# A Conformer/RWKV-7 block: the depthwise convolution's taps given a place of their own in the order of work

## The chip, the cores and the metric

The kernel runs on one core of a Trainium2 chip. The metric is the device time of one execution in microseconds. Matmuls run on TensorE (PE; PEld is its weight load), the element-wise work on VectorE (DVE), ScalarE (ACT) and GpSimd (POOL), and SyncE (SP) issues the transfers. PE has two clocks, 1.2 and 2.4 GHz; the trace's granted clock is 1.00 at the higher one.

## What is computed

One hybrid layer in float32 for a sequence of 512 and a width of 1024: a convolution branch, a recurrent branch (RWKV-7, 16 heads of 64), gates that merge them, and a feed-forward part.

```python
h = modulate(rms_norm(x, g_norm1), shift1, scale1)
u = h @ w_in
u_conv, u_rwkv, u_gate = jnp.split(u, [2 * CONV_DIM, 2 * CONV_DIM + RWKV_COLS], axis=-1)
y_conv = conformer_conv(u_conv, ...)
y_rwkv = rwkv7_mix(u_rwkv, ...)
g_conv, g_rwkv = jnp.split(jax.nn.sigmoid(u_gate), N_BRANCH, axis=-1)
merged = g_conv * y_conv + g_rwkv * y_rwkv
x = x + gate1[:, None, :] * (merged @ w_out)
h2 = modulate(rms_norm(x, g_norm2), shift2, scale2)
ff = jnp.square(jax.nn.relu(h2 @ w_ff1)) @ w_ff2
return x + gate2[:, None, :] * ff

def conformer_conv(u, conv_w, conv_b, ln_g, ln_b, w_pw, b_pw):
    za, zb = jnp.split(u, 2, axis=-1)
    z = za * jax.nn.sigmoid(zb)
    z = depthwise_causal_conv(z, conv_w, width=31) + conv_b
    z = jax.nn.silu(layer_norm(z, ln_g, ln_b))
    return z @ w_pw + b_pw

def step(S, inp):
    r_t, w_t, k_t, v_t, a_t, b_t = inp
    Sa = jnp.einsum('bhij,bhj->bhi', S, a_t)
    S = S * w_t[:, :, None, :] + Sa[..., None] * b_t[:, :, None, :] + v_t[..., None] * k_t[:, :, None, :]
    return S, jnp.einsum('bhij,bhj->bhi', S, r_t)
```

(The convolution call is shortened to its meaning.)

## The kernel before, in words

Activations lie with channels on the partitions, in blocks of 128 channels by 512 positions. Every weight product goes through `wload` and `wmul` (lines 211 to 226): SP loads 128 columns of a weight matrix (`raw`, line 213), ACT rounds them to a high part (`wH`, line 215), POOL takes the rest (`wL`, line 216), and PE makes 24 matmuls (lines 223, 224, 225), three for each of eight slices of 128, into one of three PSUM accumulators `mm`. These are called dense matmuls here, and 24 of them a block.

The recurrence is cut into 8 chunks of 64 positions and handled for 4 groups of 4 heads. For a group come, in this order: `group_k` and `group_prep` (its r, k, v and decays, and the products of a chunk's rows among themselves, lines 546 to 698, with `group_bonus`, line 701); `group_solve` (lines 704 to 736), which inverts triangles in 31 steps of two small dependent DVE operations each (lines 721, 723), ending in DVE's transpose `G.solved`; `group_solve2` (line 738), with the matmuls `sW` and `sX` (lines 747, 753); `group_chain` (line 758), the eight steps that hand the state on: matmuls `pf` (lines 767, 769), ACT's copy F (772), matmuls `pu` (776), two copies to UV, on ACT (778) and DVE (779), matmuls `pn` (784), DVE's `sp` and S (791, 792); and `group_post`. The outputs Y (lines 799, 801) stand beside the steps.

The convolution goes by 8 blocks of 128 channels. `conv_in(j)` (line 513) makes two dense blocks and the gated input `z` (three buffers; line 520 on DVE takes it from PSUM). `conv_taps(j, z)` (line 523) makes the 31 taps through `weighted_sum` (line 133): ACT writes the first tap with the bias into one PSUM accumulator `acc` (line 143), 30 DVE operations add the others (line 145), the result is stored to DRAM (line 527), and `csum` adds up the blocks for the layer norm that follows in the stage "norm" (lines 889 to 908; its root and reciprocal are lines 198 and 199).

What orders the work is a scheduler with priorities: an instruction gets its priority from its place in the program's text, `forward(section, g)` (lines 72 to 83) shifts a section by the number in the table `FORWARD`, and of the instructions that are ready each engine gets the one with the best priority; each engine then runs its list strictly in that order. `tc.issue_after(x)` holds work back until `x` stands in the order. `window` (line 857) hands out what fills the groups, by the table `WINDOWS` (line 23): "c" is a conv block, "g" a gate block, and the bar separates what stands before a group's chain from what stands behind its start. Blocks 0 and 1 of the convolution have their inputs before the first group.

## Time and profile before

| | |
|---|---|
| median of 3 runs | 1150.29 us (1146.22 to 1151.23) |
| profiled execution | 1150.57 us, span 1148.8 us |
| granted clock of PE, mean | 0.969 |
| PE busy | 1066.7 us (93% of the span) |
| DVE busy | 765.2 us (67%) |
| ACT busy | 494.8 us (43%) |
| POOL busy | 429.5 us (37%) |

The span is the time from the first to the last instruction in the trace of one execution. In the view of busy time by stage a row has the stretch, its length, then for PE, PEld, DVE, ACT and POOL the busy us with the number of instructions in brackets, then the granted clock, the share of the transfer engines and the GB/s. A row of the timeline has the start in us, the duration in us, the engine, the line, the operation, out<-in with the tiles' names, and their shapes; "x8" at its end means that eight like it are put together, and a bracket tells how long the engine had been idle and what ended that. The copies of a tile have numbers in the order of instructions, which the trace leaves out.

### The profile page before, as it was taken

Reading aid. Unit: us, or ns where it says so; the run is one execution under the profiler, and the core shown is the slowest. Engines: PE = TensorE matmul, PEld = TensorE weight load, DVE = VectorE, ACT = ScalarE, POOL = GpSimd, SP = SyncE. Lnnn points to the kernel's source line nnn. Section 1 sums busy time; section 2 is a strip of 40 time slices with the busy share of each in tenths; the row PEclk is TensorE's granted clock in tenths of the full one; section 3 lists DMA queues with packets and bytes.
Section 4 is the critical chain, followed back from the end, with each engine's and each line's share of the span. In section 5 each row is a group of like instructions: output and inputs, shape, how many; then the busy total and the mean of one; then the engine's idle time right before and its main releaser. Section 6 shows DMA issues by size and latency. Waiting matters only on the chain.

```text
span 1148.8 us, 16008 instructions
## 1 busy us (share of the span) xinstructions
PE 1066.7 (93%) x6290; PEld 818.6 (71%) x6290; DVE 765.2 (67%) x1145; ACT 494.8 (43%) x805; POOL 429.5 (37%) x237
## 2 busy tenths in 40 slices
PE   6898999998799989999979999998999999999997
PEld 5675776666566767667656777886888888888886
DVE  5878787789877898688845649788613612522545
ACT  5555534646155473365566412334413322422331
POOL 4744242243222334125431234453444444444441
PEclk9999799998899999999978999999999999999998
DMA  9622142112321125112636779952333333333332
GB/s 321 217 71 69 47 138 75 51 52 73 99 91 51 42 69 175 48 47 65 202 106 195 232 243 335 284 158 67 92 95 107 93 92 94 107 93 92 98 101 76
DMA packets 188922, 136.73 MB, mean 119 GB/s; under 512 B 5424, under 2 KB 162480, under 8 KB 188848
## 3 DMA queue, kind: packets, MB, share of 16 engines
q1 hardware_dynamic: 188848, 135.73, 38.4%
q8 instruction: 49, 0.80, 0.3%
q14 instruction: 25, 0.20, 0.1%
HBM read 121.55 MB, written 14.16 MB: 118 GB/s over the span
## 4 chain that ended last, share of the span: by engine, by line
PE 65%; DVE 19%; ACT 6%; DMA 5%; issue 3%; POOL 2%; SPq 0%; DVEq 0%; ACTq 0%; POOLq 0%
PE mm L223 16%; PE mm L224 16%; PE mm L225 16%; DVE acc L145 4%; PE pG L663 2%; ACT wH L215 1%; PE Y L801 1%; DMA adaw<-in_w_ada_dram 1%; PE Y L799 1%; PE ch L767 1%; PE ch L776 1%; DVE t2k L251 1%; PE ch L784 1%; DVE t2k L1022 1%; POOL wL L216 1%
## 5 line engine op out<-in xcount | busy, mean ns | idle before, releaser
L216 POOL TENSOR_TENSOR wL<-raw,wH 128x1024 fp32r<-128x1024 f32 x142 | 341.7, 2406 | 592.9 <-ACT wH L215 503.6
L223 PE MATMUL mm<-b,wH 128*128 128x512 f32 x720 | 292.0, 406 | 4.1 <-ACT cv L516 2.9
L225 PE MATMUL mm<-b,wL 128*128 128x512 f32 x720 | 291.0, 404 | 3.7 <-POOL wL L216 2.9
L224 PE MATMUL mm<-b,wH 128*128 128x512 f32 x720 | 291.2, 404 | 2.2 <-DVE b L1032 2.1
L215 ACT CAST wH<-raw 128x1024 fp32r<-128x1024 f32 x142 | 149.1, 1050 | 290.7 <-PE mm L224 238.9
L145 DVE SCALAR_TENSOR_TENSOR acc<-z,vt,acc 128x512 f32<-128x512 f32 x232 | 173.1, 746 | 1.8
L223 PEld LDWEIGHTS mm<-b,wH 128*128 128x128 f32 x720 | 136.9, 190 | 36.4 <-issue 3.5
L225 PEld LDWEIGHTS mm<-b,wL 128*128 128x128 f32 x720 | 137.0, 190 | 36.0 <-POOL wL L216 3.7
L224 PEld LDWEIGHTS mm<-b,wH 128*128 128x128 f32 x720 | 137.0, 190 | 33.5 <-DVE b L1032 3.5
L224 PE MATMUL mm<-g,wH 128*128 128x512 f32 x328 | 128.2, 391 | 1.2 <-DVE g L1024 0.9
L223 PE MATMUL mm<-g,wH 128*128 128x512 f32 x328 | 128.4, 391 | 0.0
L225 PE MATMUL mm<-g,wL 128*128 128x512 f32 x328 | 127.8, 390 | 0.0
L1022 DVE TENSOR_TENSOR t2k<-t2k 128x512 f32<-128x512 f32 x32 | 73.1, 2288 | 57.7 <-ACT t2k L1019 57.4
L1066 DVE SCALAR_TENSOR_TENSOR x<-mm,cols,x 128x512 f32<-128x512 f32 x31 | 23.3, 751 | 114.3 <-PE mm L225 114.3
L224 PEld LDWEIGHTS mm<-g,wH 128*128 128x128 f32 x328 | 61.6, 188 | 15.4 <-DVE g L1024 2.2
L223 PEld LDWEIGHTS mm<-g,wH 128*128 128x128 f32 x328 | 61.6, 188 | 14.0 <-ACT g L1023 1.2
L225 PEld LDWEIGHTS mm<-g,wL 128*128 128x128 f32 x328 | 61.6, 188 | 12.7 <-issue 0.2
L1023 ACT CAST g<-t2k 128x512 fp32r<-128x512 f32 x32 | 19.8, 621 | 72.7 <-DVE t2k L1022 72.7
L663 PEld LDWEIGHTS pG<-AR,BK 64*128 64x128 f32 x256 | 27.2, 204 | 14.2 <-DVE G L666 4.9
L663 PE MATMUL pG<-AR,BK 64*128 64x128 f32 x256 | 32.3, 306 | 5.1 <-DVE G L666 2.0
L1024 DVE TENSOR_TENSOR g<-t2k,g 128x512 fp32r<-128x512 f32 x32 | 23.4, 736 | 19.9 <-ACT g L1023 19.9
L723 DVE TENSOR_TENSOR Y<-tm,Y 128x126 f32<-128x126 f32 (+22 forms) x124 | 31.8, 257 | 3.4
(292 smaller groups left out, 1538.8 us busy)
## 6 DMA issues: line engine op xcount, KB each, us to landing
raw<-in_w_ff_dram SPq DMA_DIRECT2D x64, 512.0 KB, 4.1
raw<-in_w_in_dram SPq DMA_DIRECT2D x54, 512.0 KB, 3.7
adaw<-in_w_ada_dram SPq DMA_DIRECT2D x10, 1024.0 KB, 7.0
t2k<-gate SPq DMA_DIRECT2D x24, 256.0 KB, 3.8
adac<-in_w_ada_dram SPq DMA_DIRECT2D x24, 256.0 KB, 3.4
wa<-in_w_ada_dram SPq DMA_DIRECT2D x11, 512.0 KB, 5.3
gate<-cv SPq DMA_DIRECT2D x16, 256.0 KB, 2.2
raw<-in_w_pw_dram SPq DMA_DIRECT2D x8, 512.0 KB, 4.2
```

The lines of the kernel that those rows point to most:

```text
L145: dve.scalar_tensor_tensor(dst if i == n - 1 else so_far, row, col, so_far, ALU.mult, ALU.add)
L215: act.copy(wH, raw)
L216: last_low[0] = pool.tensor_tensor(wL, raw, wH, ALU.subtract)
L223: steps.append(pe.matmul(acc, wH[:, kc, :], aH(kc), start=kc == 0, stop=False))
L224: steps.append(pe.matmul(acc, wH[:, kc, :], aL(kc), start=False, stop=False))
L225: steps.append(pe.matmul(acc, wL[:, kc, :], aH(kc), start=False, stop=kc == KC - 1))
L663: pe.matmul(pgs[e][:, i, :], BK[64 * e:64 * e + 64, c, C * e:C * e + 2 * C], G.AR[64 * e:64 * e + 64, b, c, :], start=True, stop=True)
L723: dve.tensor_tensor(X[:, s + 1:32, 0:w], tv, X[:, s + 1:32, 0:w], ALU.add)
L1022: dve.tensor_tensor(t, t, t, ALU.mult)
L1023: act.copy(rH(f), t)
L1024: dve.tensor_tensor(rL(f), t, rH(f), ALU.subtract)
L1066: dve.scalar_tensor_tensor(x1(j), acc, ada[:, 40 + j:41 + j], x1(j), ALU.mult, ALU.add)
```

## The change

The taps of a conv block were traced behind two conditions: those of blocks 2 and 3 came after the taps of blocks 0 and 1, which stood in the window, and all of the window's own were held back until the group's solve had ended. The change traces a block's taps right behind its input, drops the holding back, puts the taps of blocks 0 and 1 in front of the first group, and gives all of them a section "taps" in the table, whose offset of -1000 to -300 ranks them behind what stands after them in the text; `shift=False` leaves the priorities of later text as they are.

```diff
 FORWARD = {
     "k": (10, 10, 10, 10), "solve": (127, 153, 48, -153), "window": (0, 7, -47, -43), "chain": (-98, 348, 51, 37),
-    "post": (64, 3, 0, 359), "between": (49, 49, 49, 49), "norm": (300,), "silu": (-100,), "amid": (500,),
+    "post": (64, 3, 0, 359), "between": (49, 49, 49, 49), "norm": (300,), "silu": (-100,), "amid": (500,), "taps": (-1000, -700, -500, -300),
 }
...
             j = next(blocks_c)
             zs[j] = conv_in(j)
-            if j < 4:
-                conv_taps(j - 2, zs[j - 2])
-            with tc.issue_after(G.solved.ins):
+            with forward("taps", j // 2, shift=False):
                 conv_taps(j, zs[j])
...
     for t in Sd:
         pool.memset(t, 0.0)
+    for j in range(2):
+        with forward("taps", 0, shift=False):
+            conv_taps(j, zs[j])
     with forward("k", 0):
         G = group_k(0)
```

No instruction is added or taken away. On DVE, in the middle of group 0's solve, the order of before is this (`s` holds the triangles, `Y` the PSUM tile of the inverse, `tm` a product):

```order
L721 TENSOR_TENSOR tm_1079<-s_1075,Y_1077 128x115
L723 TENSOR_TENSOR Y_1077<-tm_1079,Y_1077 128x23x5
L721 TENSOR_TENSOR tm_1079<-s_1075,Y_1077 128x110
L723 TENSOR_TENSOR Y_1077<-tm_1079,Y_1077 128x22x5
L721 TENSOR_TENSOR tm_1079<-s_1075,Y_1077 128x126
L723 TENSOR_TENSOR Y_1077<-tm_1079,Y_1077 128x21x6
```

And the order of the change at the same place (`acc` is the accumulator of the taps, `z` the input of conv block 0, `vt` the table of tap weights):

```order
L721 TENSOR_TENSOR tm_1147<-s_1143,Y_1145 128x126
L145 SCALAR_TENSOR_TENSOR acc_679<-z_455,vt,acc_679 128x512
L723 TENSOR_TENSOR Y_1145<-tm_1147,Y_1145 128x21x6
L145 SCALAR_TENSOR_TENSOR acc_679<-z_455,vt,acc_679 128x512
L721 TENSOR_TENSOR tm_1147<-s_1143,Y_1145 128x120
L145 SCALAR_TENSOR_TENSOR acc_679<-z_455,vt,acc_679 128x512
L723 TENSOR_TENSOR Y_1145<-tm_1147,Y_1145 128x20x6
L145 SCALAR_TENSOR_TENSOR acc_679<-z_455,vt,acc_679 128x512
```

Between any two operations of the solve a tap has come to stand. Of the 240 taps, 3, 22, 0 and 0 stand inside the four solves before, and 56, 54, 49 and 0 in the change; from a solve's end to the next solve's begin it is 68, 60 and 60 before, and 38, 6 and 11 in the change.

On PE, within a step of group 0's chain, the order of before is this (`mm` the dense matmuls of a gate or conv block, with the weights `wH` and `wL` and the activations `b`):

```order
L799 MATMUL Y_1620<-Sd_640,AR_764 64x128
L225 MATMUL mm_1881<-b_458,wL_1878 128x512
L223 MATMUL mm_1881<-b_458,wH_1877 128x512
L224 MATMUL mm_1881<-b_460,wH_1877 128x512
L776 MATMUL ch_1604<-F_1602,G_767 64x64 x4
L225 MATMUL mm_1881<-b_458,wL_1878 128x512
L223 MATMUL mm_1881<-b_458,wH_1877 128x512
L801 MATMUL Y_1620<-UV_765,G_767 64x64
L224 MATMUL mm_1881<-b_460,wH_1877 128x512
L225 MATMUL mm_1881<-b_458,wL_1878 128x512
L223 MATMUL mm_1881<-b_458,wH_1877 128x512
L784 MATMUL ch_1611<-UV_765,bkT_766 64x64 x4
```

The same step in the change (`pw` and `pa` are two of the next group's small decay products):

```order
L799 MATMUL Y_1620<-Sd_640,AR_832 64x128
L565 MATMUL pw_1966<-XW,w2L_1962 128x512
L565 MATMUL pa_1967<-XA,w2L_1962 128x512
L776 MATMUL ch_1604<-F_1602,G_835 64x64 x4
L801 MATMUL Y_1620<-UV_833,G_835 64x64
L784 MATMUL ch_1611<-UV_833,bkT_834 64x64 x4
```

The dense matmuls have left this step. In the change, chain 0 has none in its first five steps, then 24 in the rest; chain 1 has none in four steps, then 24; chain 2 has 9, 5, 2, 2 and 5 in its first ones, and about 50 with the products behind it. Before, the chains with the products behind them have 139, 128 and 143.

Where they have gone shows the entrance to that chain, in the change:

```order
L225 MATMUL mm_2120<-b_459,wL_2117 128x512
L747 MATMUL sW_1499<-s_1213,G_835 32x32 x32
L753 MATMUL sX_1500<-TT_1215,s_1498 32x32 x32
L564 MATMUL pw_1915<-XW,w2H_1910 128x512
L565 MATMUL pw_1915<-XW,w2L_1911 128x512
L564 MATMUL pa_1916<-XA,w2H_1910 128x512
L565 MATMUL pa_1916<-XA,w2L_1911 128x512
L776 MATMUL ch_1577<-F_1575,G_835 64x64 x4
```

Dense matmuls stand up to the first sW, where before 294 of them were issued by then, and now 432; of these, 240 instead of 102 come after the second bonus product of group 0. For groups 1 to 3 the count at the first sW goes from 617, 938 and 1248 to 744, 1053 and 1246.

## Rows read from the trace of the kernel before

**Rows 1.** The chain that ended last, by engine, share of the whole span

```profile
PE 65%; DVE 19%; ACT 6%; DMA 5%; issue 3%; POOL 2%; SPq 0%; DVEq 0%; ACTq 0%; POOLq 0%
```

**Rows 2.** Busy time by stage: PE, PEld, DVE, ACT, POOL; clock; DMA; GB/s

```profile
143.70:173.20 29.50, 28.21 (x130) 22.41 (x129) 24.90 (x73) 11.20 (x14) 13.43 (x7) 1.00 0.44 136
173.20:232.30 59.10, 58.13 (x595) 38.73 (x596) 45.77 (x76) 30.89 (x65) 12.22 (x9) 1.00 0.21 63
232.30:277.30 45.00, 39.88 (x210) 30.66 (x211) 39.70 (x56) 27.19 (x46) 19.69 (x13) 0.96 0.22 65
277.30:321.60 44.30, 31.72 (x126) 23.90 (x125) 39.11 (x98) 10.01 (x15) 10.82 (x6) 0.85 0.31 98
321.60:380.00 58.40, 57.22 (x594) 38.07 (x594) 44.90 (x73) 31.98 (x65) 12.25 (x9) 1.00 0.19 56
380.00:421.30 41.30, 37.08 (x203) 28.51 (x203) 38.65 (x51) 21.97 (x41) 16.09 (x11) 1.00 0.21 64
421.30:453.50 32.20, 30.32 (x138) 23.05 (x138) 27.73 (x77) 14.16 (x20) 11.94 (x5) 1.00 0.45 138
453.50:514.10 60.60, 59.10 (x600) 39.18 (x600) 47.39 (x76) 31.11 (x65) 14.44 (x8) 1.00 0.20 61
514.10:555.80 41.70, 39.24 (x216) 30.45 (x217) 33.47 (x47) 27.25 (x48) 17.60 (x10) 1.00 0.23 70
555.80:597.20 41.40, 32.16 (x177) 21.03 (x177) 29.05 (x80) 24.17 (x31) 21.71 (x13) 0.88 0.52 175
```

**Rows 3.** The same view of a stretch of dense matmuls alone

```profile
920.00:1000.00 80.00, 79.77 (x351) 65.61 (x351) 26.06 (x23) 23.56 (x29) 34.05 (x15) 1.00 0.34 99
```

**Rows 4.** The timeline of DVE in solves 0 and 1: start, duration, work

```profile
148.72 0.68 DVE L701 TENSOR_TENSOR t2k<-bonus,t2k 128x512 f32<-128x512 f32 x1
...
286.27 0.23 DVE L721 TENSOR_TENSOR tm<-s,Y 128x81 f32<-128x81 f32 x1
286.42 0.75 DVE L145 SCALAR_TENSOR_TENSOR acc<-z,vt,acc 128x512 f32<-128x512 f32 x1
287.08 0.24 DVE L723 TENSOR_TENSOR Y<-tm,Y 128x81 f32<-128x81 f32 x1
```

**Rows 5.** Taps alone (DVE, line 145), products 1: busy (count), clock

```profile
232.30:277.30 45.00, 20.09 (x27) 0.96 0.22 65
```

**Rows 6.** The timeline of one step of chain 0, dense matmuls left out

```profile
189.13 0.34 PE L767 MATMUL ch<-S,AR 64*64 64x64 f32 x4
...
189.95 0.27 ACT L772 COPY F<-ch 128x128 f32<-128x128 f32 x1 [0.84 <-PE ch L769]
...
190.58 0.45 PE L776 MATMUL ch<-F,G 64*64 64x64 f32 x8
...
191.08 0.26 ACT L778 COPY UV<-ch 64x128 f32<-64x128 f32 x1 [0.86 <-PE ch L776]
...
193.00 0.45 PE L784 MATMUL ch<-UV,bkT 128*64 128x64 f32 x8
...
193.50 0.29 DVE L791 TENSOR_TENSOR sp<-ch,S 128x128 f32<-128x128 f32 x1 [1.18 <-PE ch L784]
```

**Rows 7.** The timeline of chain 3's first step

```profile
604.13 0.69 PE L776 MATMUL ch<-F,G 64*64 64x64 f32 x8 [1.88 <-ACT G L734]
...
604.95 0.26 ACT L778 COPY UV<-ch 64x128 f32<-64x128 f32 x1
...
605.24 0.28 DVE L779 COPY UV<-ch 64x128 f32<-64x128 f32 x1 [5.92 <-ACT UV L778]
...
605.58 0.70 PE L784 MATMUL ch<-UV,bkT 128*64 128x64 f32 x8
```

**Rows 8.** Busy time by stage, as rows 2: a stretch before solve 0

```profile
116.00:128.00 12.00, 12.00 (x48) 9.48 (x46) 7.43 (x11) 2.99 (x7) 2.54 (x2) 0.50 0.10 30
```

**Rows 9.** The timeline of ACT in chain 0

```profile
216.64 1.28 ACT L586 ACT_TABLE_LOAD   x1
```

**Rows 10.** Waits: engine, line, releaser: total us, count, longest us

```profile
DVE nrm L199 <- ACT nrm L198: 10.7, 2, 9.7
```

## The prediction

> **What bounds the kernel now.** I read the chain of waits first. It lies on TensorE (PE) for 65% of the span and on VectorE (DVE) for 19% [rows 1], so a change on DVE pays where PE waits for it and otherwise only through what it does to PE's work. Then I cut the stretch that the change touches, 143.7 to 597.2 us, at four kinds of event: a group's first solve step, its first sW matmul, the last copy of its chain, and the next group's first solve step. The table by stage [rows 2] has one row for solve 0, chain 0, products 1, solve 1 and so on to solve 3. The reader is to see three things. In the chains PE is busy 97 to 98% at a granted clock of 1.00, because dense matmuls (the weight blocks of lines 223 to 225) fill the gaps of a chain of short dependent steps. In the products stages DVE is busy 80 to 94% of the time. The solves last from 29.5 to 44.3 us, with DVE busy 70 to 88% of that.
>
> The price of PE's filler comes from a stretch of nothing but dense work: 351 matmuls in 80 us [rows 3], 0.228 us each at the full clock, which is 2.4 GHz. The solve on DVE is a chain of 62 small operations; a tap set between two of them takes the slot in which the next must wait for the last. A pair of one solve operation and one tap starts 0.81 us after the pair before it, the tap itself lasting 0.75 [rows 4].
>
> **The change, stage by stage.** Nothing is added or removed: the same 240 DVE tap operations, the same matmuls and the same transfers run in another order, and a wait (taps behind the group's solve) is dropped. By the order of the instructions the taps inside the solves go from 3, 22, 0 and 0 to 56, 54, 49 and 0, and the taps between a solve's end and the next solve's begin from 68, 60 and 60 to 38, 6 and 11. On PE, the dense matmuls issued before the first sW go from 294, 617, 938 and 1248 to 432, 744, 1053 and 1246. In a chain and the products behind it they fall from 139, 128 and 143 to about 24, 24 and 50.
>
> *Solves 0 to 2.* Solve 0 will wait for PE. After the second bonus sum at 148.72 [rows 4] PE has 240 dense matmuls ahead of sW where it had 102. 102 x 0.228 = 23.3 us leads to 172.0, and the trace has sW at 173.2, so I add 1.2: 148.7 + 54.7 + 1.2 = 204.6, a stage of 61 us for 29.5. Solves 1 and 2 will wait for DVE. A tap between two solve operations adds 0.81 less 0.34 for the bare operation (24.90 us for 73 instructions in solve 0 [rows 2]), or 0.47 us. Solve 1 gets 32 more, 15.0 us, so 59 us; solve 2 gets 49, 23.0 us, so 55 us. If a tap hid nothing, it would cost 0.75, and those two stages 23 us more; this is one bound, and 0 (all of it in idle DVE time) is the other. I take 0.47, because it is the row of this very pair in solve 1.
>
> In these rows the operation behind a tap starts 0.66 us after a tap that lasts 0.75, before the tap has ended [rows 4]. The Trainium skill, "VectorE: DVE Perf Modes", section "The DRAIN you can't avoid", says that the next DVE operation does not start until the pipe has emptied. By that a pair would take the sum of both durations, 0.98 for 0.81, and 159 taps in solves would make the sum 27 us longer. The trace disagrees, and it decides.
>
> *Products 1 to 3.* Taps and dense matmuls leave them. 27 taps are 20.1 us of DVE's 39.7 in products 1 [rows 2, 5], and 42 of the 139 dense matmuls stood there, 9.6 us of PE's 39.9. What remains is PE at 30 us. I take 32 us for each of the three (45.0, 41.3 and 41.7 before), 33 if the clock is low at their start; the bounds are 28 (all DVE time comes off) and 45 (none does).
>
> *Chains 0 to 2.* Here the filler goes, and the question is what a bare chain lasts. One step at the full clock, start to start [rows 6]: 0.82 from the pf matmuls to the copy F, 0.34 to pu, 0.50 to the first UV copy, 0.29 to the second, 0.34 to pn, 0.50 to sp, 0.30 to S, 0.34 to the next pf. (The 0.29 and the 0.34 behind a copy are those of [rows 7], which have no dense matmul between.) That is 3.4 us. At the half clock, 1.2 GHz, pu to UV takes 0.82 for 0.50 [rows 7]; I put 0.32 on each of the three matmul groups of a step, 4.4 us. Added to eight steps are the head of a chain, 6.9 us at the half clock (597.20 [rows 2] to 604.13 [rows 7]) and an estimated 6.2 at the full one; the next group's preparation between the steps, 6 us, bounded below by two table loads of 1.28 [rows 9] and above by 8; in chain 0 the taps left, 0.9 us a step; and half of the dense matmuls left, at 0.228 or, at half the clock, about 0.45.
>
> At the full clock chain 0 is 8 x 4.3 + 6.2 + 6 + 2.7 = 49 us, chain 1 is 27.2 + 12.2 + 2.7 = 42, chain 2 is 27.2 + 12.2 + 5.7 = 45. At the half clock they are 60.7, 53.5 and 59.4. Before, they were 59.1, 58.4 and 60.6.
>
> *Which clock.* This is the choice on which the forecast turns. In the trace PE keeps 1.00 in all three chains, with about 100 dense matmuls in each [rows 2]. It has 0.50 for 12 us from 116 to 128, where it is busy all the time with a stretch of other, small matmuls and transposes [rows 8], and in the head of chain 3, whose stage before shows 0.88 and PE busy 78% [rows 2, 7]. Products 1 and solve 1 fall to 0.96 and 0.85, and these are the stages with little dense work. In the changed order chains 0 and 1 begin with four or five steps without a dense matmul, which is nearer to [rows 7, 8] than to the filled chains, so I take the half clock for chains 0 and 1. Chain 2 has 9 and 5 dense matmuls in its first steps and I put it between, at 52.
>
> The Trainium skill, "TensorE: Matmul & The Clock Gate", section "A second HAM failure mode: psum-queue depth-cycling", reports that short idle times between groups of matmuls make the clock go back and forth between its two levels. That speaks against taking the filler out of the chains; no row here shows a chain with the filler gone and the clock still to be lost, so the rule would only raise the chance of the sum above.
>
> *Solve 3.* Before, DVE waits 9.7 us in it for the square root of the norm (line 199) [rows 10], because the channel sums are ready late. With the taps done early in chain 2 the norm's matmuls are 30 to 40 dense matmuls earlier, and that wait goes: 41.4 becomes 31.7. Other queues: on SP the stores of the conv blocks stand a few places earlier, and no weight load is moved behind a later one, so I put nothing there; ScalarE (ACT) and GpSimd (POOL) are busy 21 to 65% of these stages [rows 2] and hide their moved parts. If that cover fails, it is in the solves, where a DVE operation that waits for PE holds the whole solve: DVE takes the mm accumulators (lines 264 and 520) and one of the first waits for a block that PE finishes late, about 4 to 7 us by the count of matmuls; I have left it out of the sum and put it into the second rival.
>
> **The sum**, stages in order: 61 + 60.7 + 33 + 59 + 53.5 + 33 + 55 + 52 + 33 + 31.7 = 471.9 us, where the trace has 453.5 [rows 2]: 18.4 us more. The profiled execution took 1150.57 us, 1148.8 of it the span and 1.8 around it; it stands 0.3 us above the median of 1150.29. So 1150.6 + 18.4 = 1169.0, and I forecast 1169 us. In words: the dense matmuls that filled chains now run in solves that they lengthen, and the chains do not get shorter, because the clock falls in them.
>
> **The rivals.** *The clock stays (other side).* If the bare chains still run at 2.4 GHz, the sum is 61 + 49 + 32 + 59 + 42 + 32 + 55 + 45 + 32 + 31.7 = 438.7, 14.8 us less: 1136 us. For it speaks that products 1 and 2 hold 0.96 and 1.00 with small matmuls that keep PE busy 89 to 90% of the time [rows 2]; against it, [rows 8], busy all the time at 0.50. The point from which it decides: between the two sums lie 33 us that the low clock costs; if it costs less than 15 of them, the change wins. Chance 0.25.
>
> *Stalls in the solves.* DVE holds the solve while it waits for z, kk or the accumulator acc, PE has three full accumulators behind it, and the low clock reaches into products that then stay as long as before in part. With 7 us for each of two solves and 2 us for each products stage this is 20 us on top: 1189 us. For it speaks the idle time in solve 1 today, 5.2 of 44.3 us [rows 2], with a clock of 0.85; against it, that chains empty of dense work leave more freedom to catch up. Chance 0.18.
>
> *It cancels.* The clock is low in half of the chain time: about half way, 1152 us. Products 1 at 0.96 and solve 1 at 0.85 [rows 2] show that such mixtures happen. Chance 0.15. That the change does not move what it says is excluded by the order; only its size in time is open.
>
> **How the numbers follow.** The forecast has 0.42, the rivals 0.25, 0.18 and 0.15. A measurement of this kernel can tell 0.5%, 5.8 us, from no change. Slower by more than that is the forecast and the stalls: 0.60; faster is the kept clock: 0.25; within it is the cancelling: 0.15. The range reaches from 1135, just under the kept clock's time, to 1189, that of the stalls; it leaves out the lower part of the first, about 0.11, and the upper half of the second, 0.09. Cases of both signs hold much of the chance; the forecast's own range is 1158 to 1180, from the bounds of products (28 to 36 us each) and preparation (2.6 to 8 us each).
>
> **What would show it.** Right: solves 0 to 2 near 56 to 61 us, with 50 or more taps in each; chains 0 and 1 of 53 to 60 us with a granted clock well below 1.00 and PE busy for far less than 97%; products near 33 us; no wait at line 199 in solve 3. Wrong: chains of 42 to 49 us at 1.00 (then the change is faster), or solves under 50 us, which would mean that taps cost less than 0.47 us in them, or products that stay above 40 us.

## The result, and the profile after

The changed kernel takes 1181.97 us (median of 4 runs, 1180.7 to 1188.02) against 1149.33 us before: a ratio of 1.0297, 95% interval 1.0254 to 1.034. It is slower by 3%, on the side that was forecast and by more than was forecast (1169 us), inside the range (1135 to 1189). The medians leave out one execution of hold_window, 1167.6 us, that fell into a slower state of the chip. The profiled execution took 1181.24 us, its span 1179.5, which is 30.7 us more than the span before.

Three lines of the page of the changed kernel: the busy shares, PE's granted clock in the 40 slices, and the chain that ended last.

```profile
PE 1095.1 (93%) x6290; PEld 854.9 (72%) x6290; DVE 741.9 (63%) x1145; ACT 493.7 (42%) x804; POOL 429.2 (36%) x237
...
PEclk9999999566996869999697999999999999999998
...
PE 70%; DVE 15%; ACT 7%; DMA 3%; POOL 3%; issue 2%; SPq 0%; DVEq 0%; ACTq 0%; POOLq 0%
```

DVE is recorded busy for less time than before (741.9 us for 765.2) with the same 1145 operations. PE is busy 93% of the span as before, but its clock shows fives to eights in slices 8 to 10, 13 to 15, 20 and 22, and its mean is 0.929 for 0.969. The chain of waits lies on PE for 70% now, for 65% before [rows 1].

Busy time by stage of the changed kernel, cut at the same events and in the same order as [rows 2], from solve 0 to solve 3:

```profile
137.40:199.57 62.17, 60.20 (x270) 48.90 (x268) 56.80 (x129) 19.82 (x24) 28.61 (x15) 1.00 0.43 128
199.57:258.07 58.50, 48.49 (x516) 34.70 (x516) 39.11 (x67) 26.33 (x60) 5.65 (x7) 0.68 0.09 28
258.07:298.48 40.41, 35.43 (x148) 26.39 (x149) 25.98 (x37) 23.93 (x45) 9.26 (x9) 0.67 0.08 27
298.48:361.58 63.10, 57.80 (x254) 47.14 (x252) 56.40 (x129) 16.93 (x21) 27.69 (x13) 0.99 0.41 126
361.58:413.70 52.12, 46.09 (x516) 31.84 (x516) 19.38 (x40) 26.20 (x59) 4.53 (x5) 0.75 0.06 20
413.70:446.59 32.89, 28.61 (x133) 21.70 (x133) 21.32 (x30) 18.59 (x37) 5.07 (x6) 0.69 0.07 22
446.59:508.21 61.62, 60.61 (x265) 48.67 (x264) 54.82 (x125) 20.89 (x28) 27.65 (x12) 1.00 0.44 134
508.21:557.97 49.76, 46.04 (x543) 30.70 (x543) 23.46 (x44) 27.57 (x60) 7.99 (x6) 0.97 0.12 36
557.97:592.40 34.43, 30.15 (x139) 23.57 (x140) 22.82 (x32) 22.52 (x43) 9.38 (x6) 0.70 0.10 34
592.40:626.69 34.29, 32.53 (x190) 22.88 (x189) 26.66 (x77) 22.52 (x30) 21.87 (x13) 1.00 0.61 198
```

The ten stages sum to 489.3 us for 453.5. The solves take 62.2, 63.1 and 61.6 us for 29.5, 44.3 and 32.2, chains 0 to 2 take 58.5, 52.1 and 49.8 for 59.1, 58.4 and 60.6, and products 1 to 3 take 40.4, 32.9 and 34.4 for 45.0, 41.3 and 41.7. The clock is 1.00 in the solves, and 0.67 to 0.75 in chains 0 and 1 and in all products. A measure that is used below is the lost clock: (1 - granted clock) x length. In the ten stages it rises from about 13 us to about 68 us; PE's idle time there is nearly the same (43.3 for 40.5).

Where the clock falls shows the same view of PE alone in pieces of 4 us, at the entrance to chain 0 and in it:

```profile
198.00:202.00 4.00, 1.43 (x66) 1.00 0.20 61
...
202.00:206.00 4.00, 3.52 (x66) 0.64 0.47 135
...
206.00:210.00 4.00, 3.64 (x25) 0.50 0.00 0
...
234.00:238.00 4.00, 4.00 (x37) 1.00 0.11 33
...
246.00:250.00 4.00, 2.16 (x26) 0.69 0.29 82
```

At 198 PE stands idle for 2.6 of 4 us: the solve is at its end on DVE and PE has nothing left that it could take. Then the clock falls, and up to 234 us, in the steps without dense matmuls, it is at 0.50 for most of the time (0.73 and 0.70 in the two pieces from 218 to 226) though PE is recorded busy 3.6 of 4 us in the piece shown. It is back at 1.00 where chain 0's 24 dense matmuls stand (234 to 246), and falls again behind them.

Of the waits, the one for the norm has shrunk from 9.7 [rows 10] to 4.5 us. PE waits for the next group's first transposes (line 653) for 5.0, 5.2 and 5.2 us in products 1 to 3, where before no such wait was over 1.3 us; the fourth, of 3.6 us, stands before solve 0 and was there before too. The sW matmuls wait for DVE (line 729) at the end of every solve, 1.8, 5.3 and 0.7 us in solves 0 to 2. And DVE waits in the solves for kk (line 264, the next group's k, which comes from a dense block), 3.3, 3.4 and 3.3 us, which it did not before.

```profile
PE bkt L653 <- DVE BK L629: 19.0, 4, 5.2
...
DVE kk L264 <- ACT kk L263: 11.9, 7, 3.3
...
PE sW L747 <- DVE s L729: 8.9, 4, 5.3
...
DVE nrm L199 <- ACT nrm L198: 5.5, 2, 4.5
```

### The profile page after: what moved, and what is told of

Same layout as the page of the kernel before. It is cut to its first block, busy times and chain, and to the rows that moved or that the text cites. A ratio compares the mean times of both kernels' runs of the same rounds, so it can differ in the third digit from the quotient of the medians.

```text
span 1179.5 us, 16020 instructions
## 1 busy us (share of the span) xinstructions
PE 1095.1 (93%) x6290; PEld 854.9 (72%) x6290; DVE 741.9 (63%) x1145; ACT 493.7 (42%) x804; POOL 429.2 (36%) x237
## 4 chain that ended last, share of the span: by engine, by line
PE 70%; DVE 15%; ACT 7%; DMA 3%; POOL 3%; issue 2%; SPq 0%; DVEq 0%; ACTq 0%; POOLq 0%
PE mm L223 18%; PE mm L224 18%; PE mm L225 18%; PE pG L663 3%; DVE acc L145 3%; ACT wH L215 2%; PE Y L801 1%; PE Y L799 1%; PE ch L767 1%; PE prn L183 1%; PE ch L776 1%; PE ch L784 1%; DVE t2k L1023 1%; PE ch L769 1%; PE bkt L653 1%
## 5 line engine op out<-in xcount | busy, mean ns | idle before, releaser
L223 PEld LDWEIGHTS mm<-b,wH 128*128 128x128 f32 x720 | 137.4, 191 | 31.7 <-issue 2.2
L224 PEld LDWEIGHTS mm<-g,wH 128*128 128x128 f32 x328 | 61.6, 188 | 15.3 <-DVE g L1025 2.2
L223 PEld LDWEIGHTS mm<-g,wH 128*128 128x128 f32 x328 | 61.6, 188 | 14.0 <-ACT g L1024 1.2
L225 PEld LDWEIGHTS mm<-g,wL 128*128 128x128 f32 x328 | 61.6, 188 | 12.9 <-issue 0.2
L663 PEld LDWEIGHTS pG<-AR,BK 64*128 64x128 f32 x256 | 36.1, 241 | 8.6 <-issue 3.8
L663 PE MATMUL pG<-AR,BK 64*128 64x128 f32 x256 | 41.3, 345 | 0.6 <-DVE G L666 0.4
L779 DVE COPY UV<-ch 64x128 f32<-64x128 f32 x32 | 9.0, 280 | 49.5 <-ACT UV L778 49.5
L801 PE MATMUL Y<-UV,G 128*64 128x64 f32 x256 | 32.9, 252 | 6.3 <-ACT UV L778 6.3
```

Source lines behind the costliest of these rows:

```text
L223: steps.append(pe.matmul(acc, wH[:, kc, :], aH(kc), start=kc == 0, stop=False))
L224: steps.append(pe.matmul(acc, wH[:, kc, :], aL(kc), start=False, stop=False))
L225: steps.append(pe.matmul(acc, wL[:, kc, :], aH(kc), start=False, stop=kc == KC - 1))
L663: pe.matmul(pgs[e][:, i, :], BK[64 * e:64 * e + 64, c, C * e:C * e + 2 * C], G.AR[64 * e:64 * e + 64, b, c, :], start=True, stop=True)
L801: pe.matmul(o[:, e, :], G.G[:, b, e, cc, C:2 * C], G.UV[:, b, cc, e, :], start=not cc, stop=not cc or e == 1)
```

## The experiments

Four explanations were set against each other. Theory 1: the low clock of chains and products that have lost their dense matmuls is what is lost. Theory 2: these stages are bound by latency, and the clock is a by-product. Theory 3: taps between the operations of a solve cost by themselves. Theory 4, formed later: a chain needs 50 to 60 us either way, bare at the low clock or filled at the full one. All runs with a comparison:

| run | median us | ratio to before, 95% interval | clock of the profiled run |
|---|---|---|---|
| the change | 1182.0 | 1.0297 (1.0254 to 1.0340) | 0.929 |
| front_only | 1157.0 | 1.0056 (1.0019 to 1.0093) | 0.967 |
| free_only | 1186.5 | 1.0339 (1.0300 to 1.0379) | 0.934 |
| hold_window | 1157.0 | 1.0063 (1.0035 to 1.0092) | 0.955 |
| free_group0 | 1153.9 | 1.0035 (1.0012 to 1.0058) | 0.962 |
| free_group2 | 1159.0 | 1.0086 (1.0054 to 1.0118) | 0.958 |
| no_offset | 1180.9 | 1.0276 (1.0223 to 1.0330) | 0.943 |
| fill_chain | 1186.1 | 1.0316 (1.0259 to 1.0373) | 0.956 |
| warm | 1213.4 | 1.0565 (1.0532 to 1.0598) | 0.930 |
| warm_right | 1160.0 | 1.0100 (1.0065 to 1.0135) | 0.966 |
| warm_tail | 1160.4 | 1.0065 (1.0041 to 1.0089) | 0.968 |
| before_gap | 1155.3 | 1.0054 (1.0031 to 1.0077) | 0.972 |
| hold_warm | 1140.5 | 0.9933 (0.9899 to 0.9966) | 0.983 |

### Which part of the change it is: front_only, free_only, hold_window

front_only, on the changed kernel:

```diff
-            with forward("taps", j // 2, shift=False):
+            with tc.issue_after(G.solved.ins):
                 conv_taps(j, zs[j])
```

> Of the change only the taps of conv blocks 0 and 1 in front of group 0, with their offset; the taps of the window are held behind the solve as before. By the order 34 taps stand in solve 0 and none in solves 1 and 2; before the first sW stand 89 dense matmuls more than before (138 more in the full change). Theory 1 (the loss follows the chains that are emptied of dense matmuls): only chain 0 is thinner, chains 1 and 2 are full at a clock of 1.00; the kernel is within 8 us of 1150, and solve 0 still starts some 6 us earlier than before, as in the changed kernel. Theory 3 (the taps in the solves cost by themselves, by 0.5 us each on DVE): 34 taps for 3 cost 15 us and 22 fewer in solve 1 give 10 back: about 1155 us.

free_only, on the changed kernel:

```diff
+            if j < 4:
+                conv_taps(j - 2, zs[j - 2])
             with forward("taps", j // 2, shift=False):
...
-    for j in range(2):
-        with forward("taps", 0, shift=False):
-            conv_taps(j, zs[j])
```

> The other part alone: the taps of the window are traced without being held behind the solve and with their offsets; the taps of blocks 0 and 1 stay in the window as before. 58, 54 and 49 taps in the solves by the order. Theory 1 and theory 3 alike: this part carries the loss, 1180 to 1190 us, and solve 0 starts at about 143 us as before, since the earlier start belongs to the other part. If the front part carries a loss of its own, this run is faster than the changed kernel by it.

hold_window, on the changed kernel:

```diff
-            with forward("taps", j // 2, shift=False):
+            with tc.issue_after(G.solved.ins), forward("taps", j // 2, shift=False):
                 conv_taps(j, zs[j])
```

> The changed kernel with one thing undone: the window's taps are held behind the group's solve again, but keep the offsets of the section taps. 34, 16 and 6 taps in the solves by the order, and 503, 775 and 1086 dense matmuls up to the sW of groups 0 to 2 by one count (before 414, 737, 1058; the change 552, 864, 1173). Theory 1: the loss goes by the dense matmuls pulled ahead of sW: about a quarter of it is left for groups 1 and 2, 1150 to 1160 us, with chains 1 and 2 at a clock above 0.95. Theory 3 (taps in solves at 0.5 us each): 56 for 25 taps, 15 us: 1160 to 1165 us.

The loss sits in the dropped holding back: free_only has all of it (1.034), the front part alone costs 0.6%, and holding the window's taps back again leaves 0.6%. Stages of front_only, solve 0, chain 0, solve 1 and chain 1:

```profile
137.61:188.22 50.61, 49.15 (x221) 39.73 (x219) 43.57 (x106) 17.72 (x22) 22.95 (x12) 1.00 0.45 136
188.22:243.59 55.37, 51.90 (x565) 35.39 (x565) 43.07 (x75) 28.60 (x62) 12.04 (x9) 0.91 0.16 49
291.61:319.02 27.41, 26.10 (x112) 20.59 (x112) 22.94 (x70) 9.37 (x12) 11.98 (x5) 1.00 0.51 164
319.02:377.14 58.12, 56.59 (x594) 38.19 (x594) 47.24 (x74) 31.67 (x64) 11.38 (x9) 1.00 0.18 52
```

With 34 taps in solve 0 that stage is 50.6 us for 29.5, and with none in solve 1 that one is 27.4 for 44.3. The length of the solves follows the taps from stage to stage, and chain 1, full of dense matmuls, is at 1.00 as before.

One sub-expectation fell. Solve 0 began at 137.6 us in front_only and at 138.7 in free_only, whose order on PE and DVE up to there is that of before, so the earlier start (137.4 for 143.7 in the profiled executions) is not due to the taps of blocks 0 and 1. The stretch of [rows 8] in free_only:

```profile
116.00:128.00 12.00, 11.28 (x71) 8.45 (x71) 9.95 (x16) 7.79 (x20) 2.67 (x3) 1.00 0.13 38
```

The granted clock was 1.00 there and 0.50 in the profiled execution of before: this differs from one execution to another. The 46 matmuls that start between 116 and 128 us in before take 12 us there, and 7.1 us (116.4 to 123.5) in free_only at 1.00. In both executions PE had stood idle for about 3 of the 4 us in front of them, so the same idle stretch was followed by the lower clock in one and not in the other.

### One group alone, and no offsets: free_group0, free_group2, no_offset

free_group0, on the kernel before (free_group2 has 2 for 0):

```diff
-            with tc.issue_after(G.solved.ins):
-                conv_taps(j, zs[j])
+            if j // 2 - 1 in (0,):
+                with forward("taps", j // 2, shift=False):
+                    conv_taps(j, zs[j])
+            else:
+                with tc.issue_after(G.solved.ins):
+                    conv_taps(j, zs[j])
```

> The kernel before, with the window's taps set free (no holding back, offsets of the change) in group 0 alone. 58 taps in solve 0 for 3, none in solve 1 for 22; chain 0 keeps its filler up to its sixth step and the products behind it have none, chains 1 and 2 as before. Theory 1: a loss of the products and the chain's end alone, 1152 to 1162 us, clock 0.955 to 0.965. Theory 3: 33 more taps in solves at 0.5 us: 1166 us, with no fall of the clock.

> The same in group 2 alone: 40 taps in solve 2 for none; chain 2 keeps some five dense matmuls a step in half of its steps, products 3 none, and the norm's sums are ready earlier, so the wait at line 199 in solve 3 (9.7 us before, 4.5 in the change) shrinks. Theory 1: 1152 to 1160 us, clock 0.955 to 0.965. Theory 3: 40 taps at 0.5 us less the 5 us of the wait: 1165 us.

no_offset is the changed kernel with `"taps": (0, 0, 0, 0)`.

> The changed kernel with the offsets of the section taps set to 0. By the order as many taps stand in the solves (60, 55 and 55), but the chains keep more dense matmuls: about 50 in each for 24, 24 and 50, with three to ten in each of the first steps. Theory 1: faster than the changed kernel, 1160 to 1172 us, with a mean clock near 0.945. Theory 3: the same as the changed kernel or slower, 1180 to 1188 us, since 11 more taps stand in solves.

free_group0 and free_group2 came out in theory 1's intervals (1153.9 and 1159.0 us) and under theory 3's 1166 and 1165. Solve 2, chain 2 and products 3 of free_group2, where before has 32.2, 60.6 and 41.7 at 1.00 [rows 2]:

```profile
415.19:473.49 58.30, 56.77 (x249) 44.70 (x247) 52.38 (x119) 21.67 (x29) 25.20 (x11) 1.00 0.43 133
473.49:534.05 60.56, 54.35 (x542) 35.93 (x542) 30.80 (x53) 27.22 (x60) 7.52 (x6) 0.78 0.12 37
534.05:568.98 34.93, 30.19 (x139) 23.58 (x140) 23.29 (x33) 23.11 (x44) 9.84 (x6) 0.70 0.06 21
```

The solve grows by 26 us; the chain is no shorter at 0.78, and only the products and solve 3 (34.1 for 41.4) give 7 us back each. In this chain the clock is 0.50 from 480 to 496 us though PE is recorded busy all of that time, and it had stood idle for only 0.9 of the 4 us from 472 to 476, where the solve ends. no_offset came out as theory 3 had it, 1180.9 us, where theory 1 expected 1160 to 1172. Its solve 0 and chain 1:

```profile
142.72:200.68 57.96, 45.77 (x198) 36.81 (x197) 57.96 (x131) 15.07 (x19) 21.84 (x13) 0.88 0.35 109
347.10:404.64 57.54, 56.57 (x555) 36.82 (x556) 18.98 (x39) 26.60 (x59) 6.40 (x5) 0.80 0.10 29
```

Here the solve has fewer dense matmuls, and PE stands idle in it for 12.2 of 58.0 us; the chain has a clock of 0.80 and takes 57.5 us. So the offsets of the change decide nothing, and theory 1 as stated was too narrow: a better mean clock (0.943) bought no time. In the ten stages the lost clock is about 53 us for the change's 68, but PE's idle time is 56 us for 43.

### The filler put back into the chains: fill_chain

On the changed kernel:

```diff
-WINDOWS = ("ccgg|g", "ccggg|", "cc|gggg", "ggg|ggg")
+WINDOWS = ("ccgg|g", "ccgg|g", "ccg|ggg", "ggg|ggg")
...
-                pe.matmul(px[lo:lo + 32, u // NCH, u % NCH, :], ...)
+                G.sx = pe.matmul(px[lo:lo + 32, u // NCH, u % NCH, :], ...)
...
-        with forward("k", g + 1):
+        with tc.issue_after(G.sx.ins), forward("k", g + 1):
             Gn = group_k(g + 1)
```

> The changed kernel with its filler put back into the chains: the next group's k blocks are queued behind the sX matmuls, and one gate block of windows 1 and 2 moves behind the chain's start. By the order the taps stay in the solves (58, 36 and 44), while every chain step but a few has dense matmuls again (6, 8, 3, 2, 5 ... as before), and the first sW of groups 0 to 2 comes after 432, 744 and 1080 dense matmuls (by a count in which before has 414, 737 and 1058, the change 552, 864 and 1173). Theory 1 (clock): the chains run at a granted clock of 0.95 or more and the mean clock rises from 0.929 to 0.955 or more; the time falls to 1160 us (1150 to 1172), what is left being PE's idle time in the long solves. Theory 2 (the chains are slow by latency and DVE's order): chains at 52 to 60 us and no gain, 1180 us. Theory 3 (taps in solves cost by themselves): 138 taps for 25, so the solves alone hold the loss: 1180 us or more.

A miss for theory 1, which had 1160 us: it measured 1186.1. Its solve 0, chain 0 and products 1:

```profile
136.24:194.75 58.51, 33.03 (x150) 26.41 (x148) 56.49 (x129) 13.36 (x17) 18.07 (x10) 0.82 0.33 99
194.75:254.90 60.15, 58.17 (x582) 38.98 (x582) 42.80 (x70) 30.55 (x63) 10.16 (x9) 0.92 0.13 41
254.90:288.31 33.41, 28.63 (x161) 22.54 (x160) 23.90 (x30) 18.91 (x37) 8.46 (x6) 0.95 0.11 32
```

The chain is filled and at 0.92, the products are at 0.95 and short (33.4 us), but now PE stands idle for 25.5 of the 58.5 us of solve 0, and the chain is as long as before (60.2). In the ten stages the lost clock is about 44 us for the change's 68, and PE's idle time 71.0 for 43.3. The dense matmuls are a fixed stock. The taps make three solves of some 60 us that have to be filled from it; what fills them is missing in the chains, and what fills the chains is missing in them. The run also shows what sets the length of solve 0: it takes 58.5 us with 138 dense matmuls by the trace, where the change has 258 and 62.2 us, so most of that length is DVE's chain of solve operations and taps and not PE's dense matmuls.

### Filler from outside the stock: warm, warm_right, warm_tail

Matmuls that add no result can tell whether the clock is the price, since they take nothing from the stock. The first try, `warm`, on the changed kernel (the same behind pu and pn; `ch_tile` gives the chain's tile of 128 columns and the rest of its PSUM bank):

```diff
+        def warm(t):
+            if g < 3:
+                for _ in range(2):
+                    pe.matmul(t, hH(0)[:, 0:P], hH(1)[:, 0:T - NB * C], start=True, stop=True)
...
-            pf = psum("ch", 1, (P, NB, C))
+            pf, wf = ch_tile()
...
+            warm(wf)
             Fs = atile("F", (P, NB, C), 2)
             act.copy(Fs, pf)
```

> The changed kernel, and in the chains of groups 0 to 2 two extra matmuls of 128x384 behind each of the three matmul groups of a step, into a part of the chain's PSUM bank that nobody reads: 48 or so per chain, that add no result. Theory 1 (the clock: chains and the products behind them are slow because PE falls to its lower clock when the dense matmuls are gone): the chains come back to a granted clock above 0.9, chain 0 lasts about 50 us (58.4 in the changed kernel), chain 1 about 44 (52.1), products 1 about 34 (40.5), and the kernel takes about 1158 us, between 1150 and 1168. Theory 2 (latency: the chain's steps and DVE's order set these lengths, the clock is a by-product): chains of 52 to 60 us although the clock is up, the kernel at 1180 us or, for the extra matmuls, up to 1190.

It measured 1213.4 us, a miss for both theories, and it did not make the test: the extra matmuls lie in the bank that the next copy reads, so each copy waits for them, and the clock stayed low. Chain 0 of warm and a part of it, then the timeline of a copy of F behind the extra matmuls (line 769 of that kernel):

```profile
203.63:276.23 72.60, 64.51 (x560) 43.51 (x560) 42.65 (x71) 26.60 (x60) 7.72 (x9) 0.69 0.08 26
208.00:220.00 12.00, 11.32 (x60) 6.47 (x59) 8.30 (x13) 6.81 (x14) 1.34 (x2) 0.50 0.18 59
```

```profile
217.98 1.01 PE L769 MATMUL ch<-b 128*128 128x384 f32 x2
...
219.02 0.27 ACT L782 COPY F<-ch 128x128 f32<-128x128 f32 x1 [1.35 <-PE ch L769]
```

PE is recorded busy 11.3 of 12 us at a clock of 0.50. The second try, warm_right, on the changed kernel, has the extra matmuls in the bank of the outputs Y, which no step reads (`pyt` is that bank for two steps, its second half unused; `mm` is the last matmul before; `warm(mm)` also stands behind pn and, in odd steps, behind pf):

```diff
-    def group_solve2(G):
+    def group_solve2(G, g=0):
...
+        wy = psum("Y", 1) if g < 3 else None
+        def fill(n):
+            if g < 3:
+                for _ in range(n):
+                    pe.matmul(wy, hH(0)[:, 0:P], hH(1), start=True, stop=True)
+        fill(10)
...
+        with tc.issue_after(mm.ins):
+            fill(4)
...
+        with tc.issue_after(mm.ins):
+            fill(6)
...
+        def warm(last, n=3):
+            if g < 3:
+                with tc.issue_after(last.ins):
+                    for _ in range(n):
+                        pe.matmul(pyt[:, 256:512], hH(0)[:, 0:P], hH(1)[:, 0:256], start=True, stop=True)
...
+            warm(mm)
             act.copy(G.UV[64:128, :, c, 0, :], pu[64:128])
```

> The changed kernel with extra matmuls that add no result, now in the PSUM bank of the outputs Y, so that no step of the chain waits for them: ten of 128x512 when PE stands idle at the solve's end, four behind sW, six behind sX, and three of 128x256 behind each of the three matmul groups of a chain step (groups 0 to 2). Theory 1 (the low clock in the bare chains and products is what the change loses): granted clock above 0.9 in chains 0 and 1 (0.68 and 0.75 in the change), chain 0 about 50 us, chain 1 about 46, products 31 to 36; the kernel 1155 us, between 1148 and 1166. Theory 4 (a chain needs 50 to 60 us either way: bare at the low clock, or filled at the full clock with its steps queued behind the filler; only the long solves are new): chains of 52 to 62 us though at the full clock, the kernel 1172 to 1190 us.

1160.0 us: the extra matmuls make the changed kernel 22 us faster. Solve 0, chain 0, products 1, solve 1, chain 1 and products 2 of warm_right:

```profile
140.11:202.66 62.55, 62.43 (x281) 50.80 (x279) 57.17 (x129) 19.83 (x24) 28.95 (x15) 1.00 0.42 127
202.66:253.62 50.96, 46.32 (x584) 35.60 (x583) 39.64 (x70) 26.71 (x60) 5.55 (x7) 0.93 0.08 23
253.62:290.60 36.98, 32.13 (x146) 23.84 (x147) 23.91 (x35) 23.59 (x45) 10.66 (x9) 0.77 0.13 41
290.60:350.67 60.07, 60.04 (x262) 48.75 (x261) 55.07 (x126) 15.76 (x20) 25.34 (x12) 1.00 0.42 130
350.67:393.75 43.08, 42.42 (x580) 32.46 (x580) 21.97 (x42) 26.01 (x59) 5.21 (x5) 1.00 0.09 26
393.75:429.23 35.48, 30.23 (x154) 23.08 (x152) 23.98 (x32) 22.95 (x42) 10.53 (x8) 0.81 0.08 23
```

Chains 0 and 1 are at 0.93 and 1.00 for 0.68 and 0.75, and last 51.0 and 43.1 us for 58.5 and 52.1: theory 1's numbers (50 and 46). Theories 2 and 4 fall, since a chain without its dense matmuls is short as soon as the clock is up. Chain 0 is the cleanest pair: it holds 24 dense matmuls in both runs, and 36 taps for 33. From solve 1 on the order has moved as well: chain 1 has 18 dense matmuls for 24 and products 2 have 54 for 33, so not all of the 22 us can be put down to the clock alone. The solves stay nearly as long as in the change (62.6 and 60.1).

warm_tail adds extra matmuls at the chains' end, where PE waits for line 653:

```diff
                 act.copy(Y[:, c // 2], py)
+                if c == NCH - 1:
+                    warm(mm, 28)
```

> As warm_right, and 28 more matmuls of 128x256 that add no result at the end of chains 0 to 2, where PE stands idle for some 5 us before the products (granted clock 0.77, 0.81 and 0.90 in the products of warm_right). Theory 1: the products start at the full clock and take 30 to 33 us for 37, 35 and 35, the kernel 1150 us, between 1143 and 1157. Against it: if the products are bound by DVE and ACT at their start, the clock is worth nothing there and the time stays near 1160 us.

Products 1 and 2 of warm_tail:

```profile
257.70:293.29 35.59, 33.43 (x183) 25.43 (x182) 23.87 (x35) 23.83 (x45) 10.72 (x9) 0.86 0.14 44
400.72:430.56 29.84, 26.79 (x168) 20.74 (x166) 23.76 (x32) 20.36 (x39) 7.85 (x7) 1.00 0.09 28
```

They are shorter (35.6 and 29.8 us for 37.0 and 35.5 in warm_right), and the ten stages sum to 457.7 us for 466.1. But the median is 1160.4 us, the same as that of warm_right, where 1150 was expected: in the profiled execution solve 0 begins 4.4 us later (144.5 for 140.1) and the part behind solve 3 takes 3 us more. Why that is so was not settled.

### Filler elsewhere: before_gap, hold_warm

before_gap is the kernel before with the `fill` calls of warm_right (12, 4 and 6 matmuls) in groups 1 and 3 alone.

> The kernel before with the same kind of filler only where PE idles at the end of solves 1 and 3: twelve extra matmuls of 128x512 before sW, four behind sW, six behind sX. They add no result. Theory 1: the granted clock of chain 3's head, 0.50 for some 15 us behind 596 us, rises, and that is worth 2 to 5 us: 1145 to 1148 us. Theory 4: chain 3's head is bound by the copies and the clock is worth nothing, 1150 us, or 1 to 3 us more for the extra work.

Chain 1 of before_gap, and a piece of the head of its chain 3:

```profile
323.24:387.05 63.81, 61.01 (x596) 40.46 (x596) 45.51 (x77) 30.59 (x65) 11.18 (x8) 0.95 0.16 47
606.00:622.00 16.00, 14.32 (x224) 10.12 (x225) 8.78 (x15) 13.14 (x25) 0.24 (x1) 1.00 0.57 179
```

In the first 16 us of chain 3 the clock is 1.00 (0.57 from 597 to 613 us of before), and yet the kernel is 0.5% slower, outside what either theory expected. The extra matmuls also moved the order behind them: chain 1 takes 63.8 us for 58.4 at a clock of 0.95. The run therefore does not tell what the clock in chain 3 is worth.

hold_warm puts the extra matmuls of warm_tail into hold_window (8, 3 and 4 around sW and sX, one behind each matmul group, 28 at a chain's end).

> The kernel hold_window (window's taps held behind the solve, those of blocks 0 and 1 in front) with the extra matmuls of warm_tail, one instead of three behind each matmul group of a step. It took 1158 us without them at a mean clock of 0.955 to 0.966. Theory 1: 1145 to 1152 us, since products 1 and 2 at 0.72 and 0.85 and chain 0 at 0.86 come back; and if it is under 1146, it beats both kernels. Against it, as before_gap showed: in chains that have dense matmuls the extra ones only stand in the way, 1155 to 1162 us.

It measured 1140.5 us, 0.9933 of before (0.9899 to 0.9966): 0.7% under the kernel before, and under the changed kernel. Solve 0 to chain 1:

```profile
137.36:187.94 50.58, 49.29 (x221) 39.62 (x220) 43.56 (x106) 16.64 (x21) 22.96 (x12) 1.00 0.45 136
187.94:242.45 54.51, 52.90 (x603) 38.12 (x604) 44.52 (x72) 29.35 (x62) 11.54 (x9) 1.00 0.14 40
242.45:273.73 31.28, 28.92 (x184) 21.98 (x183) 28.05 (x42) 23.81 (x45) 7.71 (x7) 1.00 0.15 44
273.73:309.56 35.83, 35.65 (x156) 28.56 (x154) 32.98 (x85) 10.88 (x14) 15.74 (x8) 1.00 0.50 157
309.56:361.11 51.55, 51.38 (x594) 36.72 (x594) 38.49 (x70) 29.47 (x63) 11.34 (x8) 1.00 0.14 42
```

With 34 and 13 taps in the first two solves by the order, those last 50.6 and 35.8 us, everything up to there is at 1.00, and these chains and products are shorter than before (54.5, 31.3 and 51.6 us for 59.1, 45.0 and 58.4). Products 3 are longer, some 56 us for 41.7, and why was not looked into. The extra matmuls are worth some 16.5 us on hold_window (1157.0 to 1140.5).

## Why the prediction was right, and where it was short

The sign and the core of the mechanism came out: the solves grow, the chains do not get much shorter, and the clock falls in them. The forecast was 18.4 us more in the ten stages, and the trace has 35.8; outside them the start came 6.3 us earlier and the end cost 1.2 more, which makes the 30.7 us of the span. Against the forecast the solves 0 to 2 took 11.9 us more, the products 8.7 more, the chains 5.8 less and solve 3 2.6 more. The earlier start was in no term, and without it the miss would have been larger: that is luck. Of the forecast's signs, chain 1 (52.1 us) lies just under its 53 to 60, the solves (61.6 to 63.1) just over their 56 to 61, the wait at line 199 did not go, and products 1 (40.4) are over the 40 that it named as a sign of being wrong.

*Solves.* Forecast 61, 59 and 55, measured 62.2, 63.1 and 61.6, with 57, 55 and 50 recorded taps. Solve 0 was to wait for PE's 240 dense matmuls. In the trace its sW matmuls wait 1.8 us for DVE, and fill_chain has 58.5 us there with far fewer dense matmuls; so the 61 came out by luck, because PE's work and DVE's were nearly equally long. For solves 1 and 2 the term that was mis-sized is 0.47 us for a tap. Over the three solves DVE's busy time rose by 76.3 us for 137 more recorded taps, 0.56 each, and its idle time by 4.6 us. The forecast took 0.34 us for the bare operation, the mean of all DVE instructions of solve 0; bare operations of the form of [rows 4] follow each other in 0.28 us in the kernel before:

```profile
150.32 0.24 DVE L721 TENSOR_TENSOR tm<-s,Y 128x81 f32<-128x81 f32 x1
150.60 0.25 DVE L723 TENSOR_TENSOR Y<-tm,Y 128x81 f32<-128x81 f32 x1
```

So a tap adds 0.53 us to the 0.28, and not 0.47 to 0.34. A pair of one operation and one tap in solve 2 of the changed kernel:

```profile
470.48 0.28 DVE L723 TENSOR_TENSOR Y<-tm,Y 128x126 f32<-128x126 f32 x1
470.67 0.75 DVE L145 SCALAR_TENSOR_TENSOR acc<-z,vt,acc 128x512 f32<-128x512 f32 x1
471.33 0.28 DVE L721 TENSOR_TENSOR tm<-s,Y 128x136 f32<-128x136 f32 x1
```

A pair takes 0.85 us here, not the 0.81 of [rows 4], since this solve operation is longer (0.28 for 0.23). The Trainium skill, "VectorE: DVE Perf Modes", section "The DRAIN you can't avoid", says that the next operation waits until the pipe is empty, but also that a next operation that is not held starts earlier, which the prediction left out. By the first sentence alone a pair would take at least the sum of both durations, 1.03 us; the trace has 0.85, so it fits the exception here as in [rows 4]. The 27 us that the prediction worked out from the first sentence count the taps of solve 0 too, which it had wait for PE; for the 81 taps that its sum adds to solves 1 and 2 they would be 14 us.

*Chains.* Forecast 60.7, 53.5 and 52 us with the half clock in chains 0 and 1 and the full one for part of chain 2, measured 58.5, 52.1 and 49.8 at 0.68, 0.75 and 0.97. This choice carried the forecast, and warm_right shows that it was right in substance: with the clock up 22 of the 32 us come back, though the order had moved a little too. The size is in part luck. The forecast had 0.50 over the whole of chains 0 and 1 and 11.7 and 11.5 us for it; the clock fell only half to two thirds as far, and between warm_right and the change a fall of 0.25 goes with 7.5 us in chain 0 and 9.0 in chain 1, more than half of what the forecast had for twice that fall. That the time goes with the clock shows among the executions of one kernel too: the ten of front_only run from 1147.8 us with 35.5 us of lost clock to 1163.7 with 53.4. What brings the clock down was not settled. I had only the missing dense matmuls; the trace also shows an idle stretch of PE at the solve's end in front of the fall (198 us), which DVE causes, and warm_right fills both. Such a stretch is neither enough (116 us, before and free_only) nor needed (chain 2 of free_group2).

The Trainium skill, "TensorE: Matmul & The Clock Gate", section "A second HAM failure mode: psum-queue depth-cycling", tells of short idle times between groups of matmuls that make the clock go back and forth; the pieces of chain 0 above show it going back and forth (0.50, 1.00, 0.69 within 50 us), but no run shows that short idle times are the reason.

*Products.* Forecast 33 each, measured 40.4, 32.9 and 34.4. Products 1 is the one term that failed by much: I had the low clock at the start alone, and in pieces of 4 us it is 0.50 for some 25 of the 40 us there (some 20 of 33 in products 2). The wait of about 5 us in front of line 653 was in no row of before either, but all three stages have it, so it does not set products 1 apart. That stage has 40 dense matmuls by the trace where the other two have 33 and 34; what makes up the rest of the 6 to 7.5 us by which it is longer was not settled.

*Solve 3.* Forecast 31.7, measured 34.3: the wait at line 199 shrank to 4.5 us and did not go.

*The rivals.* The kept clock (1136 us, chance 0.25) did not come. It was perhaps also too cheap: warm_tail, with most of the stages at or near 1.00, sums to 457.7 us, not 438.7, of which the solves, longer than forecast here too, make 7.9; how much its own extra matmuls cost is not known. With the clock kept the change would, by that sum, have won little or nothing. The stalls (1189 us, chance 0.18) came in part, and their stages sum to 491.9 us, nearer to the measured 489.3 than the forecast's 471.9. In the three solves DVE waited 15.5 us for kk, z and the accumulator, for 2.0 before; other waits fell away, which is why its idle time rose by 4.6 us only. What else lies between the forecast and the measurement is the price of a tap and products 1.

*That the dense matmuls are a stock* was in the forecast's last sentence, but I did not see how far it reaches. fill_chain and no_offset, where I trusted the clock alone, came out 14 and 9 us above the ends of theory 1's ranges, because PE then idles in the solves.

## What to carry to other kernels

Independent work between the operations of a dependent chain is not free, even on an engine with idle time: here a tap in the solve's gaps cost 0.5 to 0.6 us of a path that the chain behind it waits for. In the kernel before 122 of the 232 recorded taps lay in chains 0 to 2, beside PE's work, and taking most of them out made these chains, at their lower clock, only 0.6, 6.3 and 10.8 us shorter. Before work is moved into a gap, count what the other engine has to fill the longer stage with, and which stage that filler is then missing in. And look at the granted clock of each stage beside its busy share: PE was busy 93% of the span in both kernels, and its mean clock was 0.969 in one and 0.929 in the other.

## What the runs showed of the hardware

PE recorded busy for 11.3 of 12 us kept a granted clock of 0.50 when the matmuls came in small groups between waits (warm), and so it did for 12 of 12 us in the kernel before [rows 8]. 231 matmuls that add nothing raised the clock of chains 0 and 1 from 0.68 and 0.75 to 0.93 and 1.00 and made the changed kernel 22 us faster; 28 at a chain's end, one behind each matmul group and 15 around sW and sX in each of three groups made hold_window 16.5 us faster. The same 46 matmuls, in the same order, ran at 0.50 in 12 us in one execution and at 1.00 in 7.1 us in another; so [rows 8], on which the prediction leaned, showed one execution and not a property of the order.
